# Sixteen pairs of input projection blocks with seven products for eight, and the activation combinations on VectorE alone

## The chip, the cores and the metric

The kernel runs as one program on one core of one Trainium2 chip. The metric is the device time of one execution in microseconds; lower is better. Every time below is one of the runs shown or is read from the profile of one execution. The engines are called by their names in the profile: PE is TensorE (matmul) and PEld its weight load, DVE is VectorE, ACT is ScalarE, POOL is GpSimd, SP is SyncE, which here only issues DMAs.

## The reference

Two requests of 512 tokens each, the prompt and the sample, go through the same layer with the same weights. What matters here is the large input projection, and the convolution that uses part of it:

```python
h = rms_norm(x, norm_g)                                  # 2 x 512 tokens, D_MODEL 1024
proj = jnp.einsum('bsd,de->bse', h, w_in)
c_q, c_kv, k_rope, gate_a, conv_in, gate_c, mg_a, mg_c = split_columns(proj)
# branch A: latent attention of 8 heads, y_a = (attn * silu(gate_a)) @ w_o_attn
# branch C:
u = conv_in[..., :1024] * jax.nn.sigmoid(conv_in[..., 1024:])
u = depthwise_conv(u, kern, width 31) + dw_bias          # along the tokens
u = jax.nn.silu(layer_norm(u, conv_ln_g, conv_ln_b)) * jax.nn.silu(gate_c)
y_c = jnp.einsum('bsc,cd->bsd', u, w_pw2)
merged = jax.nn.sigmoid(mg_a) * y_a + jax.nn.sigmoid(mg_c) * y_c
return x + jnp.einsum('bsd,de->bse', merged, w_out)
```

All of it is float32.

## The kernel before

**Products.** A float32 matrix product is made of three passes in the type fp32r: both operands are split into a high and a low part, and the kernel adds high·high, high·low and low·high. The weight split is a cast on ScalarE (L128, L178) and a subtraction on VectorE or GpSimd (L129, L179).

**Blocks of the input projection.** The activations stand transposed in SBUF as eight k-blocks of 128 channels, `hH[k, b]` and `hL[k, b]`, for batch b = 0 (prompt) and 1 (sample). The projection is made in blocks of 128 output columns. Their names are `ca` and `cb` (the two halves of the convolution's gated input), `ga` and `gc` (the two SiLU gates), `ma` and `mc` (the two merge gates), each with j from 0 to 7. A block alone (`single`, matmuls at L325 into tiles `pbi`) takes 8 k-blocks × 2 batches × 3 passes = 48 matmuls of 512 columns, so two of them take 96. Two blocks together can be made by `seven`, which treats the product as a 2×2 matrix product (k halves by batches by blocks) with seven products of half size in place of eight: 7 × 4 × 3 = 84 matmuls (L356 to L358, tiles `pba`, `pbb`, `pbc`, `pbd`). For that it needs combinations of the weights, formed by `sums` on GpSimd (four adds of 128×512), which with the raw halves give seven splits (`ohi` on ScalarE at L178, `olo` on GpSimd at L179); combinations of the activations, `TH[n, k]` and `TL[n, k]` for n = 1 to 4, formed once at the beginning by `combine_x`; and five additions on the results: `u2` on GpSimd (L376) and `v`, `b`, `c`, `d` on VectorE (L382, L383, L387, L394).

**The start.** The tokens are normed (`norm_x`), transposed on PE into PSUM banks (`trans_x`, L275), and split into `hH` (ScalarE, L306) and `hL` (VectorE, L307) by `evac_x`. The first two blocks, `cb0` and `ca0`, sit in tiles `blk` and run for batch 0 while batch 1 is still being transposed, two banks at a time from the pool `p1`. `whole_x` rebuilds the float32 activations of batch 0 as `xw`. `combine_x(k)` forms, out of `xw` and the transposes of batch 1, `t1` and `t3` on VectorE (L291, L292), `t2` and `t4` on GpSimd (L293, L294), then for each of the four a high part on ScalarE (L298) and a low part on GpSimd (L299). After this the pool of `blk` is closed and PSUM is given to `pb` (6 banks, all `pbi` and `pba` to `pbd` tiles) and `py`. The first `pbi` tile takes the bank that `ca0` occupied, which becomes free with the product u = ca·sigmoid(cb) on VectorE (L494).

**The convolution.** When `ca_j` is done, `take` forms u_j (L494) and queues `conv_ops`: one ScalarE operation that starts y (L406), 30 taps on VectorE (L412, `scalar_tensor_tensor` of 128×1024; the first reads u and y from SBUF, those between accumulate in the PSUM tile `py`, the last writes y), and a DMA of y_j to DRAM (`y_s`, L414, on SP's queue). `drain(n)` puts the next n of these steps into the program between pieces of PE work.

**Order.** The list `plan` sets the order of the units on PE, which is kept as written. On the other engines a scheduler orders the instructions by priorities and modelled times. The weights stream in through three `raw` tiles by DMAs on SP's queue (L115). The last NLN = 6 units are the tail: there `tokens(t)` is woven between the halves of single blocks. It loads y back from DRAM for 128 tokens (`load_tok`: `yt` from `y_s`, L531, and `gt` from `gc_s`, L532), transposes it on PE into `yT` (L537), and does the layer norm and the gates on VectorE and ScalarE. The weights of the `p` projection, attention, and the output projection follow; they take the second half of the span.

Of the kernel before, what the change touches and what calls it, by code (L numbers as in the profile page):

```python
# [9 lines left out]
F32 = mybir.dt.float32  # L10
# [7 lines left out]
P = 128  # L18
D = 1024
S = 512  # L20
NT = 1024
KD = 8
# [21 lines left out]
def encoder_block(tc, xp_d, xs_d, win_d, wkr_d, whd_d, wqr_d, wo_d, wp_d, wout_d, vec_d, dwk_d, rg_d, rc_d, yp_d, ys_d):  # L44
    nc = tc.nc
    opened = {}

    def open_pool(name, **kw):
        if kw.get("space") is not DRAM:
            kw["reuse_waits"] = "tile"  # L50
        cm = tc.tile_pool(name=name, **kw)
        opened[name] = cm
        return cm.__enter__()
# [5 lines left out]
    f = lambda ap: ap.bitcast(F32)  # L59
    mm = nc.tensor.matmul  # L60
    ACT = nc.scalar.activation
    DVE = nc.vector
# [17 lines left out]
    pp = open_pool("pp", bufs=3, space=PSUM)  # L80
# [111 lines left out]


    plan = [("cb", 0), ("ca", 0), ("cb", 1), ("ca", 1), ("ma", 0), ("ma", 1)]
    singles = [("ga", j) for j in range(2, KD)] + [("ma", j) for j in range(2, 6)] + [("mc", j) for j in range(KD)]
    twos = [(("gc", j), ("gc", j + 1)) for j in range(0, KD, 2)] + [(("ga", 0), ("ga", 1))]
    for j in range(2, KD):
        plan.append((("cb", j), ("ca", j)))
        if j % 2 == 0:
            plan += [singles.pop(0), singles.pop(0)]  # L200
        else:
            plan.append(twos.pop(0))
    plan += twos + singles
    NLN = 6
    keys = []
# [66 lines left out]
    def trans_x(b, banks, ks):  # L272
        for tt in range(4):
            for k in ks:
                nc.tensor.transpose(banks[k][:, tt * P : (tt + 1) * P], xt[4 * b + tt][:, k * P : (k + 1) * P], identf)  # L275

    tp = open_pool("hT", bufs=1, side="right")
    TH = {(n, k): tp.tile([P, S], F32R, name=f"tH{n}_{k}") for n in (1, 2, 3) for k in range(4)}
    TL = {(n, k): tp.tile([P, S], F32R, name=f"tL{n}_{k}") for n in (1, 2, 3) for k in range(4)}
    xw = {k: tp.tile([P, S], F32, tag=f"t4_{k}", name=f"xw{k}") for k in range(KD)}  # L280

    def whole_x(k):

        nc.gpsimd.tensor_add(xw[k], f(hH[k, 0]), f(hL[k, 0]))

    def combine_x(k, banks):
        g1, g2 = (vec[:, V_NG + q : V_NG + q + 1] for q in (k, k + 4))
        b22 = xpool.tile([P, S], F32, tag="b22", name=f"b22_{k}")
        t = {n: wp.tile([P, S], F32, tag=f"s{n}", bufs=1, name=f"t{n}_{k}") for n in (1, 2, 3, 4)}
        ACT(b22, banks[k + 4], AF.Identity, scale=g2)  # L290
        DVE.scalar_tensor_tensor(t[1], banks[k], g1, xw[k], op0=ALU.mult, op1=ALU.subtract)  # L291
        DVE.scalar_tensor_tensor(t[3], banks[k], g1, b22, op0=ALU.mult, op1=ALU.subtract)  # L292
        nc.gpsimd.tensor_sub(t[2], b22, t[1])  # L293
        nc.gpsimd.tensor_sub(t[4], xw[k + 4], t[2])  # L294
        TH[4, k] = tp.tile([P, S], F32R, tag=f"t4_{k}", name=f"tH4_{k}")
        TL[4, k] = tp.tile([P, S], F32R, tag=f"t4_{k + 4}", name=f"tL4_{k}")
        for n in (1, 3, 2, 4):
            nc.scalar.copy(TH[n, k], t[n])  # L298
            nc.gpsimd.tensor_sub(TL[n, k], t[n], f(TH[n, k]))  # L299

    def evac_x(b, banks, ks):
        for k in ks:
            g = vec[:, V_NG + k : V_NG + k + 1]
            hi = hp.tile([P, S], F32R, name=f"hH{k}_{b}")
            lo = hp.tile([P, S], F32R, name=f"hL{k}_{b}")
            ACT(hi, banks[k], AF.Identity, scale=g)  # L306
            DVE.scalar_tensor_tensor(lo, banks[k], g, f(hi), op0=ALU.mult, op1=ALU.subtract)  # L307
            hH[k, b], hL[k, b] = hi, lo

    def x_bank(b, k):  # L310
        return p1.tile([P, S], F32, tag="p1", name=f"xT{b}_{k}")
# [121 lines left out]
    banks = {}  # L433
# [18 lines left out]
        block_mm(first[i], i, hh, hl, (0,))  # L452
    for k in range(KD):
        whole_x(k)
    for k in range(4):
        banks = {kk: x_bank(1, kk) for kk in (k, k + 4)}
        trans_x(1, banks, banks)
        evac_x(1, banks, banks)
        combine_x(k, banks)
    for i in (0, 1):  # L460
        block_mm(first[i], i, hh, hl, (1,))
        ensure(3 + i)
# [119 lines left out]
    pp = open_pool("pp", bufs=3, space=PSUM)  # L582
# [335 lines left out]
    ga = stage_a(*units[0])  # L918
# [35 lines left out]
    ga = {1: stage_a(*units[1])}  # L954
    gr = pieces[2:]
    for s_ in range(4 * NU + 3):
        n, j = divmod(s_, 4)
# [46 lines left out]
    pp = open_pool("pp2", bufs=4, space=PSUM)  # L1004
# [131 lines left out]
```

## Time and profile before

| | |
|---|---|
| three runs | 1182.19, 1182.81, 1184.61 us; median 1182.81 us |
| the profiled execution | 1184.55 us |
| its span in the profile | 1182.8 us |
| share of the span busy | PE 97%, DVE 65%, ACT 41%, POOL 29% |
| mean DMA rate | 92 GB/s |

The profile is of one execution, with the span counted from its first to its last instruction; the 1.75 us between span and time lie around it. A row of the trace such as `385.40 76.16 PE pbi L325 x336` is a start, a duration, an engine, a tile and line, and how many instructions it groups; square brackets at a row's end give the idle time of that engine before it and what ended it. The slices of the page cut the span into 40 parts of 29.6 us.

### The profile page before, as it was taken

The page shows a single profiled execution, that of the slowest core. Times are in us where ns is not written, and L with a number is a line of the kernel's source. Part 1 is how long each engine was busy: PE and PEld are TensorE (multiplying, and loading weights), DVE is VectorE, ACT ScalarE, POOL GpSimd, SP SyncE. Part 2 cuts the span into 40 slices and gives each one's busy share as a digit, 9 for nine tenths or more (in the row PEclk, how much of TensorE's full clock was granted, in tenths as well). Part 3 has the DMA queues.
Part 4 walks back from the last instruction along what each step waited for, and adds up shares of the span by engine and source line. Part 5 has one row for each costly group of instructions (what it writes and reads, how often), then busy time and mean ns, then how long its engine had stood idle before and what let it go on. Part 6 is the DMA issues. An engine that isn't in the chain of part 4 may idle for free.

```text
span 1182.8 us, 15035 instructions
## 1 busy us (share of the span) xinstructions
PE 1145.4 (97%) x5856; PEld 969.4 (82%) x5856; DVE 763.1 (65%) x1112; ACT 488.5 (41%) x909; POOL 343.3 (29%) x292
## 2 busy tenths in 40 slices
PE   6689999999999999999999999999999999999998
PEld 4468888888888888877888887899999998888887
DVE  5589899989999962652212454787877789344311
ACT  6522344343343222871101335776676687122200
POOL 5853566586576322200000001322122221000000
PEclk9889999999999999999999999999999999999999
DMA  6011223223223444534343012101100111344431
GB/s 253 1 54 71 71 89 111 86 71 107 89 107 107 160 147 151 158 115 160 138 142 125 23 52 76 39 26 34 35 25 19 36 36 37 107 135 166 161 107 72
DMA packets 46519, 109.52 MB, mean 93 GB/s; under 512 B 3696, under 2 KB 20336, under 8 KB 46448
## 3 DMA queue, kind: packets, MB, share of 16 engines
q1 hardware_dynamic: 41552, 91.78, 23.6%
q10 hardware_dynamic: 4896, 16.78, 3.5%
q8 instruction: 46, 0.75, 0.3%
q14 instruction: 25, 0.20, 0.1%
HBM read 79.18 MB, written 29.36 MB: 92 GB/s over the span
## 4 chain that ended last, share of the span: by engine, by line
PE 92%; POOL 3%; ACT 3%; DVE 1%; issue 1%; DMA 1%; SPq 0%; ACTq 0%; DVEq 0%
PE blk L325 22%; PE pbi L325 20%; PE po L1058 7%; PE pt L825 2%; PE pbd L356 2%; PE pba L356 2%; PE pbb L356 2%; PE pbd L358 2%; PE pba L358 2%; PE pbb L358 2%; PE pbb L357 2%; PE pbd L357 2%; PE pba L357 2%; PE pkv L733 1%; PE pkv L735 1%; PE pkv L734 1%
## 5 line engine op out<-in xcount | busy, mean ns | idle before, releaser
L412 DVE SCALAR_TENSOR_TENSOR py<-u,dwk,py 128x1024 f32<-128x1024 f32 x224 | 288.5, 1288 | 6.2
L128 ACT CAST whi<-raw 128x1024 fp32r<-128x1024 f32 (+3 forms) x59 | 60.5, 1025 | 282.0 <-PE blk L325 165.8
L325 PE MATMUL pbi<-hH,whi 128*128 128x512 f32 x352 | 138.9, 395 | 8.1 <-DVE u L494 8.1
L325 PE MATMUL pbi<-hL,whi 128*128 128x512 f32 x352 | 137.9, 392 | 0.0
L325 PE MATMUL pbi<-hH,wlo 128*128 128x512 f32 x352 | 108.9, 391 | 0.0
L129 DVE TENSOR_TENSOR wlo<-raw,whi 128x1024 fp32r<-128x1024 f32 (+2 forms) x38 | 53.4, 1405 | 59.9 <-ACT whi L128 59.9
L325 PEld LDWEIGHTS pbi<-hH,whi 128*128 128x128 f32 x352 | 66.6, 189 | 22.1 <-DVE u L494 8.5
L325 PEld LDWEIGHTS pbi<-hH,wlo 128*128 128x128 f32 x352 | 66.5, 189 | 14.0
L325 PEld LDWEIGHTS pbi<-hL,whi 128*128 128x128 f32 x352 | 66.7, 190 | 13.6
L179 POOL TENSOR_TENSOR olo<-s,ohi 128x512 fp32r<-128x512 f32 x44 | 57.5, 1318 | 52.7 <-ACT ohi L178 52.7
L129 POOL TENSOR_TENSOR wlo<-raw,whi 128x1024 fp32r<-128x1024 f32 x20 | 48.4, 2418 | 83.5 <-ACT whi L128 83.5
L325 PE MATMUL blk<-a,whi 128*128 128x512 f32 x256 | 68.4, 389 | 0.0
L816 ACT ACTIVATE pr<-sc,nm,sqs 128x512 f32<-128x512 f32 x64 | 51.2, 800 | 28.3 <-DVE nm L814 28.2
L251 POOL TENSOR_TENSOR rk<-sk,mhalf 128x4 f32<-128x4 f32 x16 | 17.2, 1074 | 147.7 <-DVE sk L743 147.7
L325 PE MATMUL blk<-hH,whi 128*128 128x512 f32 x144 | 57.6, 406 | 1.2 <-ACT hH L306 0.7
L325 PE MATMUL blk<-hL,whi 128*128 128x512 f32 x144 | 57.8, 401 | 0.5 <-DVE hL L307 0.4
L178 ACT CAST ohi<-s 128x512 fp32r<-128x512 f32 x44 | 26.2, 620 | 75.2 <-PE pbi L325 51.0
L325 PEld LDWEIGHTS blk<-a,whi 128*128 128x128 f32 x256 | 48.0, 188 | 9.9
L179 POOL TENSOR_TENSOR olo<-raw,ohi 128x512 fp32r<-128x512 f32 x33 | 43.7, 1324 | 35.2 <-ACT ohi L178 26.5
L325 PE MATMUL blk<-cH,whi 128*128 128x512 f32 x128 | 50.7, 396 | 2.4 <-ACT whi L128 2.4
L1061 DVE TENSOR_TENSOR o<-po,xr 128x1024 f32<-128x1024 f32 (+1 forms) x9 | 10.0, 1106 | 64.2 <-PE po L1058 64.2
L603 DVE TENSOR_TENSOR tmc<-blk,smc 128x1024 f32<-128x1024 f32 x8 | 9.8, 1225 | 64.2 <-PE blk L325 64.2
(272 smaller groups left out, 3076.5 us busy)
## 6 DMA issues: line engine op xcount, KB each, us to landing
raw<-in_win_dram SPq DMA_DIRECT2D x53, 512.0 KB, 3.6
y_s<-y SPq DMA_DIRECT2D x8, 512.0 KB, 4.0
ga_s<-stga ACTq DMA_DIRECT2D x8, 512.0 KB, 2.6
gc_s<-stgc ACTq DMA_DIRECT2D x8, 512.0 KB, 2.6
yt<-y_s SPq DMA_DIRECT2D x8, 512.0 KB, 5.3
gt<-gc_s SPq DMA_DIRECT2D x8, 512.0 KB, 4.1
mc_s<-stmc ACTq DMA_DIRECT2D x8, 512.0 KB, 3.4
raw<-in_wp_dram SPq DMA_DIRECT2D x8, 512.0 KB, 5.1
```

Of the source, the lines that this page charges most:

```text
L128: nc.scalar.copy(hv, rv)
L129: (sub or DVE).tensor_sub(lv, rv, f(hv))
L178: nc.scalar.copy(hi[:, sl], src)
L179: nc.gpsimd.tensor_sub(lo[:, sl], src, f(hi[:, sl]))
L325: mm(ps[b] if isinstance(ps, list) else ps[:, b], (wlo if wl_ else whi)[:, k], xl(k, b) if xl_ else xh(k, b), start=(k == 0 and wl_ == 0 a ...
L356: mm(ps, hi[:, k], xh, start=first and k == 0, stop=False, skip_group_check=not first)
L357: mm(ps, hi[:, k], xl, start=False, stop=False, skip_group_check=not first)
L358: mm(ps, lo[:, k], xh, start=False, stop=k == 3, skip_group_check=not first)
L412: DVE.scalar_tensor_tensor(out, u[:, :, i : i + S], dwk[:, j, i : i + 1], src, op0=ALU.mult, op1=ALU.add)
L816: ACT(pr, ps, AF.Exp, bias=nm, scale=r["sq"][:, j : j + 1], accum_out=sm)
L825: nc.tensor.transpose(pt[:, kt], pr[:, kt * P : (kt + 1) * P], identf)
L1058: mm(ps[:, n], lhs[k][:, ts_], w[k][:, n * S : (n + 1) * S], start=first_, stop=last_)
```

## The change

It has three parts. `plan` now makes 16 units by `seven` instead of 11: to the six pairs (`cb_j`, `ca_j`) for j = 2 to 7 and the four of `gc` come all four of `ga` (one before) and two of `mc`. Each of the six pairs is now followed by one such two; before, a pair with even j was followed by two single blocks. Singles in `plan` after the first six units go from 18 to 8 (`ma2` to `ma5`, `mc4` to `mc7`); four twos and two singles stand between the last pair and the tail of six singles, where two twos and six singles stood. In `combine_x` all subtractions of `t2`, `t4` and of the low parts go from GpSimd to VectorE, 24 instructions. And `combine_x(k)` now runs one step behind the transposes; for odd k the two banks of the transposes come from the third tile of the pool `pp` instead of from `p1`. After the change the lines between the old L203 and L449 stand 3 lines earlier, those behind it 4 later.

```diff
     plan = [("cb", 0), ("ca", 0), ("cb", 1), ("ca", 1), ("ma", 0), ("ma", 1)]
-    singles = [("ga", j) for j in range(2, KD)] + [("ma", j) for j in range(2, 6)] + [("mc", j) for j in range(KD)]
-    twos = [(("gc", j), ("gc", j + 1)) for j in range(0, KD, 2)] + [(("ga", 0), ("ga", 1))]
+    singles = [("ma", j) for j in range(2, 6)] + [("mc", j) for j in range(4, KD)]
+    twos = [((nm, j), (nm, j + 1)) for nm, n in (("gc", KD), ("ga", KD), ("mc", 4)) for j in range(0, n, 2)]
     for j in range(2, KD):
         plan.append((("cb", j), ("ca", j)))
-        if j % 2 == 0:
-            plan += [singles.pop(0), singles.pop(0)]
-        else:
-            plan.append(twos.pop(0))
+        plan.append(twos.pop(0))
     plan += twos + singles
     NLN = 6
...
         DVE.scalar_tensor_tensor(t[3], banks[k], g1, b22, op0=ALU.mult, op1=ALU.subtract)
-        nc.gpsimd.tensor_sub(t[2], b22, t[1])
-        nc.gpsimd.tensor_sub(t[4], xw[k + 4], t[2])
+        DVE.tensor_sub(t[2], b22, t[1])
+        DVE.tensor_sub(t[4], xw[k + 4], t[2])
...
         for n in (1, 3, 2, 4):
             nc.scalar.copy(TH[n, k], t[n])
-            nc.gpsimd.tensor_sub(TL[n, k], t[n], f(TH[n, k]))
+            DVE.tensor_sub(TL[n, k], t[n], f(TH[n, k]))
...
-    for k in range(4):
-        banks = {kk: x_bank(1, kk) for kk in (k, k + 4)}
-        trans_x(1, banks, banks)
-        evac_x(1, banks, banks)
-        combine_x(k, banks)
+    held = {}
+    for k in range(5):
+        if k < 4:
+            if k % 2:
+                two = pp.tile([P, 2, S], F32, tag="pp", name=f"xT1_{k}")
+                held[k] = {k: two[:, 0], k + 4: two[:, 1]}
+            else:
+                held[k] = {kk: x_bank(1, kk) for kk in (k, k + 4)}
+            trans_x(1, held[k], held[k])
+            evac_x(1, held[k], held[k])
+        if k > 0:
+            combine_x(k - 1, held[k - 1])
```

**How the order moves.** At three places the prediction rests on it. Names in the rows are tiles with running numbers; `out<-in`.

The first place is VectorE at the end of the start, up to the u of the block `ca0` (`u<-blk,sig`) that frees the first bank of `pb`. Before:

```order
L307 SCALAR_TENSOR_TENSOR hL_1_470<-xT_3_459,vec,hH_1_469 128x512
L307 SCALAR_TENSOR_TENSOR hL_1_474<-xT_7_460,vec,hH_1_473 128x512
L291 SCALAR_TENSOR_TENSOR t_3_478<-xT_3_459,vec,xw_151 128x512
L292 SCALAR_TENSOR_TENSOR t_3_480<-xT_3_459,vec,b_3_477 128x512
L129 TENSOR_TENSOR wlo_555<-raw_552,whi_554 128x1024
L494 TENSOR_TENSOR u_583<-blk_312,sig_580 128x512 x2
L412 SCALAR_TENSOR_TENSOR py_651<-u_583,dwk,y_649 128x1024
```

and after the change, from the last `hL` on:

```order
L304 SCALAR_TENSOR_TENSOR hL_1_452<-xT_3_438,vec,hH_1_451 128x512
L291 TENSOR_TENSOR t_2_459<-xw_154,t_2_457 128x512
L296 TENSOR_TENSOR tL_2_142<-t_2_457,tH_2_130 128x512
L288 SCALAR_TENSOR_TENSOR t_3_476<-xT_3_438,vec,xw_151 128x512
L289 SCALAR_TENSOR_TENSOR t_3_478<-xT_3_438,vec,b_3_475 128x512
L296 TENSOR_TENSOR tL_2_466<-t_2_459,tH_2_465 128x512
L290 TENSOR_TENSOR t_3_477<-b_3_475,t_3_476 128x512
L296 TENSOR_TENSOR tL_3_139<-t_3_476,tH_3_127 128x512
L296 TENSOR_TENSOR tL_3_147<-t_3_478,tH_3_135 128x512
L291 TENSOR_TENSOR t_3_479<-xw_155,t_3_477 128x512
L296 TENSOR_TENSOR tL_3_143<-t_3_477,tH_3_131 128x512
L129 TENSOR_TENSOR wlo_553<-raw_550,whi_552 128x1024
L498 TENSOR_TENSOR u_581<-blk_312,sig_578 128x512 x2
```

All but one of the 24 moved subtractions now stand on VectorE ahead of that u; from the first `hL` of batch 1 to u there are 16 `scalar_tensor_tensor`, 23 such subtractions, one `wlo` and the two u. On GpSimd none of them is left.

The second place is VectorE at the end of the last unit by `seven`, whose last addition is `pbd<-pbd,u`. Before:

```order
L394 TENSOR_TENSOR pbd_2845<-pbd_2845,u_2848 128x512
L412 SCALAR_TENSOR_TENSOR py_2526<-u_2218,dwk,py_2526 128x1024 x5
L412 SCALAR_TENSOR_TENSOR y_2524<-u_2218,dwk,py_2526 128x1024
L412 SCALAR_TENSOR_TENSOR py_2840<-u_2518,dwk,y_2838 128x1024
L412 SCALAR_TENSOR_TENSOR py_2840<-u_2518,dwk,py_2840 128x1024 x28
L412 SCALAR_TENSOR_TENSOR y_2838<-u_2518,dwk,py_2840 128x1024
L542 BN_STATS bst_3464<-yT_3455 128x6 x2
```

After:

```order
L384 TENSOR_TENSOR pbc_3206<-pbc_3206,v_3209 128x512
L409 SCALAR_TENSOR_TENSOR py_2997<-u_2570,dwk,py_2997 128x1024 x3
L391 TENSOR_TENSOR pbd_3205<-pbd_3205,u_3208 128x512
L409 SCALAR_TENSOR_TENSOR py_2997<-u_2570,dwk,py_2997 128x1024 x21
L409 SCALAR_TENSOR_TENSOR y_2995<-u_2570,dwk,py_2997 128x1024
L546 BN_STATS bst_3562<-yT_3553 128x6 x2
```

Behind the last unit by `seven` 36 convolution taps stood, and now 22 stand, ahead of the first layer norm statistics of the tail.

The third place is SP's queue at the same point, where the last y goes out (`y_s<-y`) and the first tokens come back (`yt<-y_s`). Before:

```order
L115 DMA raw_3474<-in_win_dram 128x1024
L414 DMA y_s<-y_2838 128x1024
L521 DMA rg<-in_rg_dram 128x256
L522 DMA rc<-in_rc_dram 128x512
L531 DMA yt_3385<-y_s 128x8x128
L532 DMA gt_3386<-gc_s 128x8x128
L115 DMA raw_3624<-in_win_dram 128x1024
L531 DMA yt_3389<-y_s 128x8x128
```

After:

```order
L115 DMA raw_3722<-in_win_dram 128x1024
L115 DMA raw_3872<-in_win_dram 128x1024
L411 DMA y_s<-y_2995 128x1024
L525 DMA rg<-in_rg_dram 128x256
L526 DMA rc<-in_rc_dram 128x512
L535 DMA yt_3483<-y_s 128x8x128
L536 DMA gt_3484<-gc_s 128x8x128
L535 DMA yt_3487<-y_s 128x8x128
```

The two last weight loads for the tail have moved ahead of the last y, and the first two token loads follow one another. On PE, seven single blocks stood between the last unit by `seven` and the first `yT`, and three stand there now; from the first layer norm on, every engine has its instructions in the order of before.

## The prediction

> **What bounds the kernel now.** I read the page first, for the share of each engine and its course over the span:
>
> ```profile
> PE 1145.4 (97%) x5856; PEld 969.4 (82%) x5856; DVE 763.1 (65%) x1112; ACT 488.5 (41%) x909; POOL 343.3 (29%) x292
> ...
> PE   6689999999999999999999999999999999999998
> ...
> DVE  5589899989999962652212454787877789344311
> ...
> POOL 5853566586576322200000001322122221000000
> PE 92%; POOL 3%; ACT 3%; DVE 1%; issue 1%; DMA 1%; SPq 0%; ACTq 0%; DVEq 0%
> ```
>
> PE is full from the fourth slice on and carries 92% of the chain that ended last. But VectorE is nearly full in the first 14 slices (to 414 us), which are the stretch that changes. So fewer matmuls shorten the time only where VectorE and what hangs on it keep up. Then I asked what PE waits for between 50 and 540 us, followed the chain there, and asked for the clock in single stretches:
>
> ```profile
> PE pbi L325 <- DVE u L494: 8.1, 1, 8.1
> PE blk L325 <- ACT whi L128: 2.4, 1, 2.4
> ...
> 64.88 45.80 PE pbi L325 x192
> ...
> 385.40 76.16 PE pbi L325 x336
> 461.56 0.87 PE yT L537 x8
> ...
> 64.80:69.30 4.50, 4.42 (x11) 3.55 (x12) 3.07 (x4) 1.75 (x2) 2.04 (x2) 0.52 0.60 228
> 533.40:536.70 3.30, 3.19 (x8) 2.54 (x9) 1.22 (x1) 0.06 (x1) 0.00 (x0) 0.50 0.91 297
> 310.00:385.00 75.00, 75.00 (x332) 62.14 (x331) 69.36 (x64) 31.00 (x51) 54.81 (x42) 1.00 0.31 106
> ```
>
> The first two rows are waits (total, times, longest), then come three of the chain (start, duration), then three stretches (PE busy with its matmuls, weight loads, VectorE, ScalarE, GpSimd, the granted clock, DMA share, GB/s). In the whole projection PE waits once, 8.1 us for u at the end of the start, and later 2.4 us for a weight cast. After each wait the clock is about half (0.52, 0.50); elsewhere it is 1.00.
>
> **Fewer matmuls.** Five more pairs save 12 matmuls each, 60. A matmul costs its pitch, 76.16 / 336 = 0.2267 us, not the 389 ns that single ones show, since they overlap. 60 × 0.2267 = **13.6 us** less, if PE stays full. The stretch 310 to 385 is already a row of sevens, with PE busy for 75.00 of 75.00 us, so one seven lasts 84 × 0.2267 = 19.04 us. The change makes the row 16 long, and GpSimd and VectorE must finish their share within 19.04 us each time:
>
> ```profile
> 316.48 1.29 POOL L147 TENSOR_TENSOR s<-raw 128x512 f32<-128x512 f32 x1
> ...
> 335.52 1.29 POOL L147 TENSOR_TENSOR s<-raw 128x512 f32<-128x512 f32 x1
> ...
> 162.47 0.69 DVE L382 TENSOR_TENSOR v<-pa,pbb 128x512 f32<-128x512 f32 x1 [2.40 <-PE pbb L358]
> ...
> 181.51 0.69 DVE L382 TENSOR_TENSOR v<-pa,pbb 128x512 f32<-128x512 f32 x1 [0.25 <-PE pbb L358]
> ...
> 189.67 0.70 DVE L394 TENSOR_TENSOR pbd<-pbd,u 128x512 f32<-128x512 f32 x1 [0.97 <-PE pbd L358]
> ...
> 200.74 0.68 DVE L382 TENSOR_TENSOR v<-pa,pbb 128x512 f32<-128x512 f32 x1
> ```
>
> GpSimd starts its first sum once per 19.04 us; it has 12 operations of about 1.27 us there, 15.2 us. VectorE starts v of a pair at 162.47, of the two behind it at 181.51 (it had waited 0.25 us for PE) and of the next unit at 200.74 (no wait): a pair with 14 taps and two u fills 18.8 of 19.04 us, and a two, which waited 0.97 us for PE at `d`, some 18.2. So both keep pace with little to spare. I charge nothing here; PE's cover is that v is not what it waits for at once, and a lag that grew would be the third rival.
>
> **The start.** The wait of 8.1 us in front of 64.88 is the u that stood behind a weight subtraction:
>
> ```profile
> 32.00 0.75 DVE L307 SCALAR_TENSOR_TENSOR hL<-xT,vec,hH 128x512 fp32r<-128x512 f32 x1 [1.14 <-ACT hH L306]
> 32.67 0.74 DVE L291 SCALAR_TENSOR_TENSOR t<-xT,vec,xw 128x512 f32<-128x512 f32 x1
> 33.33 0.74 DVE L307 SCALAR_TENSOR_TENSOR hL<-xT,vec,hH 128x512 fp32r<-128x512 f32 x1
> ...
> 51.60 0.75 DVE L291 SCALAR_TENSOR_TENSOR t<-xT,vec,xw 128x512 f32<-128x512 f32 x1 [2.21 <-POOL t L293]
> ...
> 56.54 7.09 DVE L129 TENSOR_TENSOR wlo<-raw,whi 128x1024 fp32r<-128x1024 f32 x1 [2.96 <-ACT whi L128]
> 63.55 1.28 DVE L494 TENSOR_TENSOR u<-blk,sig 128x512 f32<-128x512 f32 x2
> ...
> 55.28 2.52 POOL L299 TENSOR_TENSOR tL<-t,tH 128x512 fp32r<-128x512 f32 x2
> 57.76 1.26 POOL L293 TENSOR_TENSOR t<-b,t 128x512 f32<-128x512 f32 x1
> 58.98 2.34 POOL L129 TENSOR_TENSOR wlo<-raw,whi 128x1024 fp32r<-128x1024 f32 x1
> 61.28 1.26 POOL L299 TENSOR_TENSOR tL<-t,tH 128x512 fp32r<-128x512 f32 x1
> ...
> 975.73 1.29 DVE L952 TENSOR_TENSOR a<-attn,a 128x512 fp32r<-128x512 f32 x2
> ...
> L129 DVE TENSOR_TENSOR wlo<-raw,whi x38: 957/1216/7086, 12.5 to 1092.9; 128x1024 fp32r<-128x1024 f32 x29, 128x896 fp32r<-128x896 f32 x8, 128x768 fp32r<-128x768 f32 x1
> ```
>
> That subtraction took 7.09 us, against a median of 1216 ns, while GpSimd worked without a gap from 55.28 to 62.54; it ended 1.1 us behind that, which is about its own normal length. The Trainium skill says why that may be ("GPSIMD Engine Reference", section "8. Key points"): GpSimd shares its SBUF interfaces with VectorE and contends with instructions of two SBUF inputs; the trace agrees here.
>
> After the change VectorE has from 32.00 on, in a row: 16 of its `scalar_tensor_tensor` at a pitch of 0.66 us (32.00, 32.67, 33.33), 10.6; 23 subtractions of two SBUF operands at about 0.61 (half the 1216 ns of a `wlo`; the pair at 975.73 gives 0.64), 14.0; `wlo` 1.2; u 1.3. That is 27.1, so u ends at 59.1 without a gap. GpSimd has nothing in between, so the 7.09 is gone. VectorE will not be gapless, as it takes each high part from ScalarE and the waits of before were 0.5 to 3 us each; I add 0.8 us. PE restarts at 59.9 instead of 64.88: **5.0 us** less. Bounds: 5.8 if gapless (59.1 against 64.88), 3.5 with 2.3 us of gaps. The transposes' new tile and the combination one step later cost PE nothing, as the last `hL` stands about 8 us ahead of u's end, where PE did its last 24 matmuls of `ca0` in 7.87 us before.
>
> **The tail.** PE reaches the first `yT` after three singles, not seven; the tokens it transposes come by a chain that begins with VectorE's last taps:
>
> ```profile
> 385.51 0.70 DVE L394 TENSOR_TENSOR pbd<-pbd,u 128x512 f32<-128x512 f32 x1
> 386.12 6.58 DVE L412 SCALAR_TENSOR_TENSOR py<-u,dwk,py 128x1024 f32<-128x1024 f32 x5
> ...
> 432.48 1.28 DVE L412 SCALAR_TENSOR_TENSOR y<-u,dwk,py 128x1024 f32<-128x1024 f32 x1
> 462.48 1.30 DVE L542 BATCH_NORM_STATS2 bst<-yT 128x6 f32<-128x512 f32 x2 [28.71 <-PE yT L537]
> ...
> 433.79 0.33 SPq L414 DMA_DIRECT2D y_s<-y  x1
> ...
> 438.08 0.38 SPq L531 DMA_DIRECT2D yt<-y_s  x1
> ...
> yt<-y_s SPq DMA_DIRECT2D x1, 512.0 KB, 4.3
> ```
>
> Before, 36 taps run from 386.12 to 433.76, 1.323 us each; y goes out at 433.79; `yt` is issued 4.29 us later, when y has landed, and takes 4.3 us: tokens at 442.4. PE comes at 461.56, so 19.2 us are to spare. After, four singles fewer bring PE 192 × 0.2267 = 43.5 us earlier against that end, and 14 taps fewer bring the tokens 14 × 1.323 = 18.5 us earlier. 19.2 − 43.5 + 18.5 = −5.8: **PE waits 5.8 us** (bounds 5.0 and 6.6, as a landing may differ by 0.8). The last weight load, now ahead of y in SP's queue, needs the tile that GpSimd frees when it splits three blocks ahead: by the order, about 25 us behind the last seven, against 30 for y, so it costs nothing. The VectorE idle of 28.71 us is what is eaten up.
>
> A wait this long also slows the clock. In 64.80 to 69.30 eleven matmuls took 4.42 us where 2.5 were due, 1.9 lost; in 533.40 to 536.70 eight took 3.19 where 1.8 were due, 1.4. I take **1.9 us** (1.4 to 2.1). The Trainium skill ("TensorE: Matmul & The Clock Gate", Part 1) has the clock halved after an idle window of about 3.4 us and whole again after as long a busy one; by it the loss would be 1.7 us, and the half clock after only 2.4 us of wait here differs from it. The start's restart is cold before and after, so that cancels.
>
> **Sum.** −13.6 − 5.0 + 5.8 + 1.9 = −10.9. The profiled execution of 1184.55 us (1182.8 span and 1.75 around) becomes 1173.7. It stands 1.74 above the median of 1182.81, so on the median: **1171.9 us**. By the bounds of the terms, 1169.8 (5.8, 5.0, 1.4) to 1174.4 (3.5, 6.6, 2.1).
>
> **Rivals.**
>
> First, no wait in the tail: something holds PE back before it by as much, or y comes earlier. 1171.9 − 7.7 = 1164.2. For it: 28.71 us of idle on VectorE. Against: the 22 taps are behind the last seven in its own order. 0.07.
>
> Second, the start gains nothing: ScalarE and VectorE hand each high and low part to one another, and the gaps add up to 5 us and more; the row at 51.60 above, 2.21 of waiting for a `t`, shows such a gap. 1171.9 + 5.0 = 1176.9. Against: what that gap waited for was GpSimd, which is now out of the loop. 0.11.
>
> Third, sevens in a row lose a little each: VectorE has 0.2 us to spare in a pair. If each of 16 loses 0.5 us, 8.0 in all: 1179.9. Against: the full row from 310. 0.10.
>
> Fourth, slower: the first tap of each convolution reads u and y from SBUF, as the 7.09 us subtraction read two operands there, and GpSimd now has sums and splits for every unit, not for eleven among singles. Of this the trace has a mild case:
>
> ```profile
> 348.04 2.23 DVE L412 SCALAR_TENSOR_TENSOR py<-u,dwk,y 128x1024 f32<-128x1024 f32 x1
> ...
> 349.13 2.28 POOL L179 TENSOR_TENSOR olo<-raw,ohi 128x512 fp32r<-128x512 f32 x1
> ```
>
> If each of the seven first taps behind the start lost 5.9 us as at 56.54, VectorE would lose 41, of which two sevens' slack of about 0.45 us each takes back 6; PE waits for v and the banks: 1171.9 + 35 = 1206.9. It decides the sign from 10.9 us, about 2.5 us at each. Against: even the row above lost 0.95 us only, as GpSimd pauses several times in 19 us. 0.05.
>
> **Chances.** Forecast 0.64, rivals 0.07, 0.11, 0.10, 0.05, others 0.03. A measurement of this kernel tells about 0.2%, 2.4 us, from no change. The range 1164.0 to 1179.0 takes in the first and second rival and part of the third. Faster 0.89 (all but the fourth and what is left of the third), same 0.05, slower 0.06.
>
> **What would show it.** The profile after should have: PE restarting near 60 us with no `wlo` of 7 us on VectorE ahead of it; 16 rows of v, 19.0 us apart, with no wait of PE between; then a wait of PE at the first `yT` of 5 to 7 us for the load of `yt`, and a half clock of about 4 us behind it. Wrong would be the forecast if v's distance grew beyond 19.2 us, if `wlo` or first taps stretched, or if u came at 63 again.

## The result, and the profile after

The changed kernel took 1172.22 us (median of 4 runs, 1170.4 to 1175.04), the kernel before 1183.35 us (median of 4 runs, 1182.19 to 1184.61). The ratio is 0.9908, 95% interval 0.9882 to 0.9934: faster by 11.1 us. The profiled execution took 1175.04 us with a span of 1173.3 us, 2.8 us above the median; where that comes from is told at the end.

The waits of PE between 50 and 540 us of the changed kernel (total, times, longest):

```profile
PE yT L541 <- DMA yt<-y_s: 4.4, 1, 4.4
PE pbi L322 <- DVE u L498: 3.7, 1, 3.7
PE blk L322 <- ACT whi L128: 2.4, 1, 2.4
```

The wait for u at the start has gone from 8.1 to 3.7 us, and a new wait of 4.4 us stands at the first `yT`, for the load of the tokens. No wait lies between them: the row of 16 sevens has none. VectorE at the end of the start, where the `wlo` is back to a normal length and the subtractions run without a gap:

```profile
32.52 0.75 DVE L304 SCALAR_TENSOR_TENSOR hL<-xT,vec,hH 128x512 fp32r<-128x512 f32 x1 [1.25 <-ACT hH L303]
...
55.70 0.69 DVE L291 TENSOR_TENSOR t<-xw,t 128x512 f32<-128x512 f32 x1
56.30 0.69 DVE L296 TENSOR_TENSOR tL<-t,tH 128x512 fp32r<-128x512 f32 x1
57.25 1.23 DVE L129 TENSOR_TENSOR wlo<-raw,whi 128x1024 fp32r<-128x1024 f32 x1 [0.25 <-ACT whi L128]
59.16 1.29 DVE L498 TENSOR_TENSOR u<-blk,sig 128x512 f32<-128x512 f32 x2 [0.68 <-ACT sig L491]
```

Then the tail. VectorE, from the last addition of the last seven to the first layer norm statistics:

```profile
411.84 0.70 DVE L391 TENSOR_TENSOR pbd<-pbd,u 128x512 f32<-128x512 f32 x1
412.45 27.78 DVE L409 SCALAR_TENSOR_TENSOR py<-u,dwk,py 128x1024 f32<-128x1024 f32 x21
440.26 1.28 DVE L409 SCALAR_TENSOR_TENSOR y<-u,dwk,py 128x1024 f32<-128x1024 f32 x1
450.77 1.30 DVE L546 BATCH_NORM_STATS2 bst<-yT 128x6 f32<-128x512 f32 x2 [9.22 <-PE yT L541]
```

SP's issues of the last y and of the first tokens:

```profile
441.57 0.33 SPq L411 DMA_DIRECT2D y_s<-y  x1
...
444.56 0.38 SPq L535 DMA_DIRECT2D yt<-y_s  x1
```

The chain (start, duration), with the restart at the start and the tail:

```profile
60.51 46.59 PE pbi L322 x192
...
441.57 2.91 DMA y_s<-y
...
444.56 4.10 DMA yt<-y_s
...
448.79 1.94 PE yT L541 x8
450.73 6.22 PE pbi L322 x24
```

And the stretches behind both waits (PE busy, then the other engines; the granted clock is the third number from the end):

```profile
60.40:65.00 4.60, 4.50 (x11) 3.53 (x12) 3.91 (x4) 1.80 (x3) 2.38 (x1) 0.50 0.37 118
448.70:452.00 3.30, 3.21 (x12) 2.95 (x13) 1.23 (x2) 0.00 (x0) 1.52 (x3) 0.51 1.03 340
```

VectorE's last tap ends at 441.54, the first tokens are there at 448.7 (444.56 + 4.10). PE had come 4.4 us earlier, and after the wait its clock is at 0.51: the eight transposes take 1.94 us where they took 0.87 before, the 24 matmuls 6.22 where such a row takes 5.49 at full clock.

### The profile page after: what moved, and what is told of

It is laid out like the page before. It is cut to its first block, busy times and chain, and to the rows that moved or that the text cites. A ratio compares the mean times of both kernels' runs of the same rounds, so it can differ in the third digit from the quotient of the medians.

```text
span 1173.3 us, 15056 instructions
## 1 busy us (share of the span) xinstructions
PE 1136.8 (97%) x5796; PEld 962.9 (82%) x5796; DVE 784.7 (67%) x1156; ACT 504.2 (43%) x944; POOL 365.6 (31%) x318
## 4 chain that ended last, share of the span: by engine, by line
PE 88%; DVE 7%; ACT 2%; DMA 1%; issue 1%; POOL 1%; SPq 0%; ACTq 0%; DVEq 0%
PE blk L322 23%; PE pbi L322 9%; PE po L1062 7%; DVE py L409 4%; PE pbd L355 2%; PE pba L355 2%; PE pbb L355 2%; PE pbd L354 2%; PE pbb L354 2%; PE pba L354 2%; PE pba L353 2%; PE pbd L353 2%; PE pbb L353 2%; PE pt L829 2%; PE pkv L737 1%; PE pkv L738 1%
## 5 line engine op out<-in xcount | busy, mean ns | idle before, releaser
L179 POOL TENSOR_TENSOR olo<-s,ohi 128x512 fp32r<-128x512 f32 x64 | 82.2, 1301 | 21.8 <-ACT ohi L178 21.6
L322 PE MATMUL pbi<-hH,whi 128*128 128x512 f32 x192 | 77.5, 404 | 3.7 <-DVE u L498 3.7
L322 PE MATMUL pbi<-hL,whi 128*128 128x512 f32 x192 | 76.3, 397 | 0.0
L179 POOL TENSOR_TENSOR olo<-raw,ohi 128x512 fp32r<-128x512 f32 x48 | 62.3, 1299 | 37.5 <-ACT ohi L178 27.8
L178 ACT CAST ohi<-raw 128x512 fp32r<-128x512 f32 x48 | 29.8, 621 | 98.1 <-POOL s L154 29.2
L178 ACT CAST ohi<-s 128x512 fp32r<-128x512 f32 x64 | 38.2, 620 | 59.6 <-POOL s L148 21.6
L322 PE MATMUL pbi<-hH,wlo 128*128 128x512 f32 x192 | 60.1, 394 | 0.0
L322 PE MATMUL blk<-cL,whi 128*128 128x512 f32 x128 | 50.3, 393 | 0.0
L322 PE MATMUL blk<-hH,wlo 128*128 128x512 f32 x144 | 49.2, 405 | 0.9 <-DVE wlo L129 0.9
L353 PE MATMUL pba<-hH,ohi 128*128 128x512 f32 x128 | 49.8, 389 | 0.0
```

The lines of the kernel that those rows point to most:

```text
L178: nc.scalar.copy(hi[:, sl], src)
L179: nc.gpsimd.tensor_sub(lo[:, sl], src, f(hi[:, sl]))
L322: mm(ps[b] if isinstance(ps, list) else ps[:, b], (wlo if wl_ else whi)[:, k], xl(k, b) if xl_ else xh(k, b), start=(k == 0 and wl_ == 0 a ...
L353: mm(ps, hi[:, k], xh, start=first and k == 0, stop=False, skip_group_check=not first)
```

## The experiments

All were timed against the kernel before on the same chip: 1183.75 us in the first group, 1184.24 in the second, 1183.91 in the third. Where a place of two traces is compared, its time is counted from the first `hL` of batch 1 (32.00 in the kernel before, 32.52 in the changed one), since the time up to there, in which x is loaded, differs by up to 2 us between executions. Differences in us are of medians, and the ratios, which come from all runs, can put them up to 2 us off.

**The plan alone.** The edit is the first hunk of the change, nothing else.

> The plan with 16 pairs alone, the start as in the kernel before. If the terms are separate and add up, as the forecast says: 60 matmuls less are 13.6 us, the wait at the first yT and the slow clock behind it give back 4.4 and 1.9 us (as the changed kernel's trace shows them), so about 7.3 us less than the kernel before, 1176. The wait for u at the start should stay near 8 us. If a row of 16 sevens needs the activation combinations on VectorE, or the gain is the start's in truth, it is 3 us or less.

1179.11 us, ratio 0.9946 (0.9931 to 0.9962): 4.6 us less by the medians and 6.4 by the ratio, where 7.3 were forecast; the interval reaches from 4.5 to 8.2. The chain of its trace:

```profile
64.01 45.99 PE pbi L322 x192
...
451.47 1.94 PE yT L534 x8
...
511.67 10.71 PE pbi L322 x47
```

and the waits of PE:

```profile
PE pbi L322 <- DVE u L491: 9.5, 1, 9.5
...
PE yT L534 <- DMA yt<-y_s: 4.2, 1, 4.2
```

The wait at the start is still there (9.5), the one in the tail is 4.2, and none lies between. The last piece of the tail starts at 511.67 where it started at 520.14 before: 8.5 us, of which 0.9 is an earlier arrival of x; 7.6 remain, which is the sum of the terms. In this execution 2.8 us of them went behind the tail, in code that is the same (1177.1 − 511.67 against 1182.8 − 520.14), where its clock fell at more places than in the kernel before (last section). So the terms of the plan stand in the trace; the time of its six runs does not by itself tell 4.6 from 7.3.

**The start alone.** The other hunks of the change, with the old plan.

> The new start alone (all combinations on VectorE, one step behind the transposes, odd k in the third tile), the plan with 11 pairs as before. By the forecast's theory PE restarts about 4.4 us earlier, some 0.8 of which a longer slow clock may take back: 3.6 to 5 us less than before, 1178.5 to 1179.8. If the earlier restart is lost again, because VectorE then sets the pace of the convolution and of the tail, there is no difference.

1179.58 us, ratio 0.9952 (0.9934 to 0.9969): 4.2 us less. In its trace PE restarts 27.13 us behind the first `hL`, not 32.88, and the first `yT` is 7.7 us earlier by the same count; 2.0 of these come from the clock, which in this execution did not fall to half behind the wait for u (last section). It is the fastest of the six, 1174.65 us. The earlier restart is not lost again. By the ratios the plan (6.4 us) and the start (5.7 us) add up to 12.1 us, where the changed kernel gained 10.9 in its first group and 12.8 when it was run again.

**The two halves of the start.** First the 24 subtractions on VectorE, but the old loop:

```diff
-        nc.gpsimd.tensor_sub(t[2], b22, t[1])
-        nc.gpsimd.tensor_sub(t[4], xw[k + 4], t[2])
+        DVE.tensor_sub(t[2], b22, t[1])
+        DVE.tensor_sub(t[4], xw[k + 4], t[2])
...
-            nc.gpsimd.tensor_sub(TL[n, k], t[n], f(TH[n, k]))
+            DVE.tensor_sub(TL[n, k], t[n], f(TH[n, k]))
```

> Of the new start only the move of the 24 subtractions to VectorE; the combination stays in step with the transposes, which use two banks as before; the plan as before. The last low part of batch 1 then stands ten rows later on VectorE, about 52.4 us, and PE has some 8 us of ca0 behind it: restart at 62 us, a gain of 2 to 3 us (1180.5 to 1181.5). If the move alone is what counts, the gain is that of the whole new start, about 4 us; if the step behind is what counts, none.

1180.79 us, ratio 0.9964 (0.995 to 0.9979): 3.0 us less, as forecast. Then the other half alone, the combination one step behind (the last hunk of the change), with the subtractions left on GpSimd:

> Of the new start only the combination one step behind the transposes and the third tile; the subtractions stay on GpSimd; the plan as before. GpSimd is as long at work as before, and the weight subtraction of VectorE that took 7.09 us still meets it: restart between 62 and 66 us, a gain of 0 to 2 us (1181.4 to 1183.4). If the wait of before came from the banks of the transposes, and not from GpSimd and VectorE sharing, PE restarts near 60 and 4 us are gained.

1187.84 us, ratio 1.0028 (1.0018 to 1.0037): 4.1 us slower, a miss for both theories. VectorE in its trace:

```profile
48.81 9.03 DVE L129 TENSOR_TENSOR wlo<-raw,whi 128x1024 fp32r<-128x1024 f32 x1 [3.38 <-ACT whi L128]
57.77 0.74 DVE L291 SCALAR_TENSOR_TENSOR t<-xT,vec,xw 128x512 f32<-128x512 f32 x1
58.43 0.73 DVE L292 SCALAR_TENSOR_TENSOR t<-xT,vec,b 128x512 f32<-128x512 f32 x1
66.76 1.29 DVE L501 TENSOR_TENSOR u<-blk,sig 128x512 f32<-128x512 f32 x2 [7.59 <-ACT sig L494]
```

and GpSimd beside it:

```profile
54.28 1.26 POOL L294 TENSOR_TENSOR t<-xw,t 128x512 f32<-128x512 f32 x1
55.51 1.25 POOL L299 TENSOR_TENSOR tL<-t,tH 128x512 fp32r<-128x512 f32 x1
59.23 3.71 POOL L299 TENSOR_TENSOR tL<-t,tH 128x512 fp32r<-128x512 f32 x3 [2.47 <-ACT tH L298]
```

and ScalarE, whose casts stand ahead of the sigmoid in its row:

```profile
58.54 1.80 ACT L298 CAST tH<-t 128x512 fp32r<-128x512 f32 x3 [5.28 <-DVE t L291]
64.20 0.62 ACT L298 CAST tH<-t 128x512 fp32r<-128x512 f32 x1 [3.86 <-POOL t L293]
```

The weight subtraction now stands ahead of the last combination on VectorE and takes 9.03 us. It ends at 57.84, 1.08 us after GpSimd's row without gaps (56.76), and only then does VectorE make the last `t`, on which ScalarE and GpSimd wait; the sigmoid for u comes behind them. In the kernel before, that subtraction also ended 1.09 us behind GpSimd's gapless row of subtractions (63.63 and 62.54). There GpSimd did not pause but went on to six memsets, which have no input tile, and its next subtraction was itself longer than its usual 1.26 us:

```profile
62.49 0.12 POOL L490 MEMSET u<- 128x30 f32 x1
...
62.86 1.90 POOL L299 TENSOR_TENSOR tL<-t,tH 128x512 fp32r<-128x512 f32 x1
```

Each time VectorE's instruction got its own 1.1 us when GpSimd's row of two-operand instructions broke off. So the step behind cost time with the subtractions on GpSimd. With them on VectorE it brings the restart from 29.31 us behind the first `hL` (subtractions alone) to 27.13 (both); the times, 3.0 and 4.2 us, lie too close to tell the two apart by themselves.

**GpSimd takes that one subtraction.** The kernel before with

```diff
-                    split(i, nc.gpsimd if i >= 4 else None)
+                    split(i, nc.gpsimd if i >= 3 else None)
```

> The kernel before with one edit: the subtraction of the fourth weight block, the one that took 7.09 us on VectorE ahead of u, is made on GpSimd. If that row alone held u, u now waits for ScalarE's sigmoid, which ended at 62.1: PE restarts 1.5 us earlier, 1182 to 1183. If GpSimd's work on the combinations holds u by another way (ScalarE's casts wait for it), there is no gain, and the 2.4 us more on GpSimd may even show.

1182.28 us, ratio 0.9981 (0.9969 to 0.9994): 1.6 us less. u now waits for the sigmoid and PE restarts 30.96 us behind the first `hL`, not 32.88. The 7 us did not vanish but struck the next VectorE instruction with two SBUF operands, the first tap (VectorE's rows):

```profile
62.70 1.29 DVE L494 TENSOR_TENSOR u<-blk,sig 128x512 f32<-128x512 f32 x2 [8.00 <-ACT sig L487]
67.33 7.55 DVE L412 SCALAR_TENSOR_TENSOR py<-u,dwk,y 128x1024 f32<-128x1024 f32 x1 [3.34 <-ACT y L406]
```

This tap too ended 1.1 us after a break in GpSimd's row, one of only 0.08 us (73.79 to 73.87). It was harmless there, since nothing on PE waited for it.

**The cover of the 24 subtractions taken away.** The prediction let them run at full pace because GpSimd is idle meanwhile. Here the changed kernel gives GpSimd work again:

```diff
+        rv = rt.rearrange("p a b c -> p (a b c)")
+        for q in range(6):
+            nc.gpsimd.tensor_add(rv[:, 0:S], f(hH[k, 1]), f(hL[k, 1]))
         DVE.tensor_sub(t[2], b22, t[1])
```

> The changed kernel with 24 additions of 128x512 more on GpSimd at the start (six for each combination; their result is overwritten and not used), so that GpSimd works there again while VectorE does its 23 subtractions of two SBUF operands. If VectorE's instructions with two SBUF operands are held off as long as GpSimd runs without a gap, as the 7.09 us of one of them suggest, several groups of up to 7 us each come on top: PE restarts 10 to 20 us later and the time is 1182 to 1192. If the two engines merely slow one another a little, or that row had another cause, it is 0 to 3 us more than the changed kernel.

1184.18 us, ratio 1.0006 (0.9994 to 1.0017): the whole gain of the change is gone, 12 us against the changed kernel (the two were timed on different chips, each beside the kernel before). PE restarts 40.4 us behind the first `hL`, where it was 28.0. The way was another than I had expected. VectorE in the middle of it:

```profile
42.12 0.74 DVE L307 SCALAR_TENSOR_TENSOR hL<-xT,vec,hH 128x512 fp32r<-128x512 f32 x1
...
45.20 1.78 DVE L293 TENSOR_TENSOR t<-b,t 128x512 f32<-128x512 f32 x1
46.91 3.49 DVE L299 TENSOR_TENSOR tL<-t,tH 128x512 fp32r<-128x512 f32 x2
50.32 1.74 DVE L294 TENSOR_TENSOR t<-xw,t 128x512 f32<-128x512 f32 x1
```

and GpSimd, 17 of the additions in a row:

```profile
32.13 28.14 POOL L292 TENSOR_TENSOR rt<-hH,hL 128x512 f32<-128x512 f32 x17 [2.76 <-DVE hL L307]
```

No instruction was held for 7 us. Of the 23 subtractions ahead of u, 16 took 1.1 to 1.8 us, not 0.68, together 13 us more, which is the later restart; the seven others took about 0.68, six of them after GpSimd's row had ended at 65.4. GpSimd's additions took 1.66, not 1.26: the two took turns. Instructions with a PSUM operand (`hL`, 0.74) were not touched.

**The tail: the same steps, half a single later.** Tokens start 24 matmuls (5.44 us) later and everything behind keeps its distance.

```diff
         for n, u in enumerate(tail[1:]):
-            tokens(2 * n)
-            take(*u, single(lambda: tokens(2 * n + 1)))
+            if n > 0:
+                tokens(2 * n - 1)
+            take(*u, single(lambda: tokens(2 * n)))
```

The changed kernel itself was run beside it.

> The changed kernel once more, so that the next three are compared with it on the same chip: about 11 us less than before, 1170 to 1175.

> The changed kernel with every token step of the tail half a single block later (5.44 us of PE work), so that the first yT comes after the load that PE waited 4.4 us for. If that wait and the slow clock of 1.9 us behind it are the price of the tail, both go; at the other end only 5.4 us of matmuls are left behind the last token, whose chain through ScalarE and VectorE took 8.9 us, so 3 to 4.5 us come back there: 1 to 3 us less than the changed kernel. If the tail is bound by its loads all along, the wait only moves to a later token and nothing is gained.

The changed kernel: 1172.39 us, ratio 0.9892 (0.9874 to 0.9911). The shifted one: 1167.18, ratio 0.9854 (0.9838 to 0.9871), 5.2 us less. The wait at `yT` is gone, and the wait at the beginning of the next stage, 2.4 us in the changed kernel, is 3.9 here (waits of PE):

```profile
PE blk L322 <- ACT whi L128: 3.9, 1, 3.9
PE pbi L322 <- DVE u L498: 3.7, 1, 3.7
```

So 1.5 us came back, not 3 to 4.5: I had put ScalarE's chain behind the last token end to end, and a part of it ran beside the wait that was there already.

**The tail: later and closer.** The first token step 5.44 us later, the others three or four k-blocks apart, the last where it was; `single` takes a table that says ahead of which k-block a token step stands.

```diff
...
+        at = [4, 8, 11, 15, 18, 22, 25, 29, 32]
         for n, u in enumerate(tail[1:]):
-            tokens(2 * n)
-            take(*u, single(lambda: tokens(2 * n + 1)))
+            take(*u, single({at[t] - 8 * n: t for t in range(9)}))
```

> The changed kernel with the first token step of the tail 5.44 us of PE work later and the other eight closer together (3 or 4 k-blocks between them, not 4), so that the last stands where it stood. If the wait of 4.4 us and the slow clock behind it (1.9) are a price of the place alone, both are saved: 6 us less than the changed kernel, 1165 to 1167. If loads, ScalarE or VectorE cannot keep a token each 6.5 us, waits come back later and 0 to 3 us are gained.

1166.45 us, ratio 0.9847 (0.9832 to 0.9861): 5.9 us less than the changed kernel. The first `yT` finds its tokens, there is no half clock behind it, and PE's waits in the whole tail are 0.9 us together, none over 0.5. The chain:

```profile
448.20 0.87 PE yT L542 x8
449.08 5.49 PE pbi L322 x24
454.57 0.87 PE yT L542 x8
456.32 4.13 PE pbi L322 x18
```

**A pair more.** 17 sevens, made of `mc4` and `mc5`:

```diff
-    singles = [("ma", j) for j in range(2, 6)] + [("mc", j) for j in range(4, KD)]
-    twos = [((nm, j), (nm, j + 1)) for nm, n in (("gc", KD), ("ga", KD), ("mc", 4)) for j in range(0, n, 2)]
+    singles = [("ma", j) for j in range(2, 6)] + [("mc", j) for j in range(6, KD)]
+    twos = [((nm, j), (nm, j + 1)) for nm, n in (("gc", KD), ("ga", KD), ("mc", 6)) for j in range(0, n, 2)]
```

> The changed kernel with one pair more (17 by seven products; mc4 and mc5 too), so one seven and one single stand ahead of the first yT where three singles stood. 12 matmuls less are 2.7 us. If VectorE's convolution sets the time of the first yT, PE only waits longer there, 7 to 8 us for 4.4, and the time stays that of the changed kernel within 1 us. If PE still sets it, 2.7 us are gained.

1175.45 us, ratio 0.9919 (0.9904 to 0.9934): 3.1 us slower by the medians than the changed kernel with 12 matmuls fewer, though the two intervals overlap; the traces show it more clearly. Its wait of PE at the first `yT`:

```profile
PE yT L541 <- DMA yt<-y_s: 10.3, 1, 10.3
```

and VectorE behind its last seven:

```profile
429.74 0.69 DVE L391 TENSOR_TENSOR pbd<-pbd,u 128x512 f32<-128x512 f32 x1
430.35 10.55 DVE L409 SCALAR_TENSOR_TENSOR py<-u,dwk,py 128x1024 f32<-128x1024 f32 x8
440.93 1.28 DVE L409 SCALAR_TENSOR_TENSOR y<-u,dwk,py 128x1024 f32<-128x1024 f32 x1
```

Its first `yT` comes 418.3 us behind the first `hL`, against 416.0 in the changed kernel run beside it: 2.3 us later, and four additions more on VectorE are 4 × 0.60 = 2.4 us. So the theory that VectorE sets the first `yT` holds, but I had missed that in that case the pair's own additions lengthen VectorE's part. In the changed kernel the path to the first `yT` runs over VectorE, and a pair more shortens PE's part, which no longer counts there.

**17 pairs with later tokens.** The two put together, with the token steps at k-blocks 8, 11, 15, 18, 22, 25, 29, 32 and 36:

> 17 pairs, and the first token step of the tail 10.9 us of PE work later, with 3 or 4 k-blocks between token steps and the last half a single block later than in the changed kernel. The wait of 10.3 us should go, 2.7 us of matmuls are saved against the spread kernel with 16 pairs, and about 1.5 us come back at the end of the tail, as in the shifted kernel: 1164.5 to 1166.5. If VectorE's convolution, which a pair more delays by 2.4 us, still sets the first yT, it is 1167 or more.

1165.41 us, ratio 0.984 (0.9827 to 0.9853): the fastest, 18.5 us below the kernel before. Its 1.0 us on the version with 16 pairs lies inside the intervals of both. The wait of 10.3 is gone; the wait at the next stage is 4.8.

## Why the prediction was right

It said 1171.9 in a range of 1164.0 to 1179.0 and a gain of 10.9 us; measured were 1172.22 and 11.1. Its terms by the trace of the changed kernel:

| term | forecast | measured | from |
|---|---|---|---|
| 60 matmuls fewer | −13.6 | −13.6 | 107.10 to 444.4 is 1488 × 0.2267 us; no wait in it |
| the start | −5.0 | −4.9 | restart less first `hL`: 32.88 before, 27.99 after |
| wait at the first `yT` | +5.8 | +4.4 | waits of PE |
| slow clock behind it | +1.9 | +1.8 | 1.94 − 0.87 and 6.22 − 5.49 |
| clock at the restart | 0 | +0.8 | 46.59 − 45.80 |
| first `hL` | 0 | +0.5 | 32.52 − 32.00 |
| behind the tail | 0 | +1.5 | 664.15 − 662.66 |
| sum | −10.9 | −9.5 | spans: 1173.3 − 1182.8 |

The start came out as summed: VectorE has just two gaps between the first `hL` and u, 0.25 and 0.68 us, 0.9 for the 0.8 of the forecast. The second is a wait for ScalarE's sigmoid, so VectorE's queue was the limit to within 0.7 us. (The forecast read VectorE as nearly full in the first 14 slices; its row has a 5 in the first two, and the start, into which the 24 subtractions went, lies in the second.)

The forecast of the wait at `yT` was too large by 1.4 us, outside its bounds of 5.0 and 6.6: it took the landing of y from the kernel before, 4.29 us from issue to issue, and it took 2.99 here. Taps (last tap ended 29.8 us behind the last seven, as worked out) and load (4.10 for 4.3) were right. The change itself shortened the landing. In the kernel before, SP had issued a weight load at 432.11, 1.7 us ahead of y, and the landing took 4.2 us; in the two other traces with that distance (the start alone, the step behind alone) it took 4.1. Wherever the load was issued 3.0 us or more ahead of y, it took 2.6 to 3.0, and in the changed kernel, where the weight loads moved ahead of y, it was 4.9 us ahead and had landed (no DMA ran in the last 1.4 us before y). That the load is the cause is read from these traces, not tested by itself. The forecast saw that move, but asked only whether it cost something.

The last three rows I had set at nothing. The first `hL` and the stretch behind the tail differ between executions. The clock at the restart does not belong to this execution alone: the 192 matmuls took 45.6 to 46.0 us in the four traces with the combinations left on GpSimd and 46.2 to 46.6 in five of the seven with the whole new start (45.20 and 43.82 in the two others), so the half clock before and after, which I let cancel, did not quite.

The near agreement of the totals is thus in part luck. The named terms give −12.3 us by the trace, the three unnamed ones give 2.8 back; and the two profiled executions stand 1.2 and 2.8 us above their medians, so that their −9.5 us are the −11.1 of the medians. Each named term came within 1.4 us of its own.

The first rival (no wait in the tail) fell with the wait. The second (the start gains nothing) fell with the start alone, 4.2 us. The third (sevens in a row lose a little) fell: PE shows no wait in 16 of them. The fourth had the right mechanism, as the runs with the step behind alone and with GpSimd kept at work show, and the wrong place: the eight first taps took 1.28 to 2.38 us in the changed kernel,

```profile
L409 DVE SCALAR_TENSOR_TENSOR py<-u,dwk,y x8: 1280/1436/2381, 63.5 to 398.7; 128x1024 f32<-128x1024 f32 x8
```

so the worst of them lost 1.1 us; that GpSimd's pauses are what keeps it so small was not tested. With GpSimd kept at work at the start the same mechanism cost 12 us and turned the change into none, so the sign did hang on it: on the 24 subtractions, which I had covered by GpSimd's idleness without a rival that tried the cover.

## What to carry to other kernels

When an engine's share of a stage is near full, count what its queue still holds when the stage ends: here PE's saving of 13.6 us was real, and 6 of it waited at the next stage for convolution taps, y's way through DRAM and a slow clock. Such a price lies in the place of the consumer, not in the amount of work, and moving the first consumer by 5.4 us of other work won it back. Before work is moved between VectorE and GpSimd, look which instructions of VectorE with two SBUF operands will run beside a busy GpSimd: the same subtraction took 1.2, 7.1 or 9.0 us.

## What the runs showed of the hardware

**VectorE beside GpSimd.** VectorE's `wlo` and first taps, 128x1024 with two SBUF operands, were held through several instructions of GpSimd (7.09, 9.03, 7.55 us) and ended 1.1 us after its row of two-operand instructions broke off, but the 128x512 subtractions beside a gapless GpSimd took turns with it (1.1 to 1.8 us). The Trainium skill ("GPSIMD Engine Reference", section "8. Key points") names the contention, and these runs agree; that section does not tell when an instruction is held through and when they alternate, and no run here settles it.

**The clock after a short wait.** The same wait of 3.7 us for u left the clock at half in the changed kernel (11 matmuls in the window above) and at full in the kernel with the start alone:

```profile
58.20:62.70 4.50, 4.50 (x20) 3.73 (x21) 3.87 (x3) 1.70 (x3) 2.40 (x1) 1.00 0.40 130
```

Behind the tail, at three places of code that all these kernels share, the clock falls to about half for a few us or does not: both profiles of the changed kernel have all three, the kernel before has two, the plan alone all three and a fourth, the subtractions alone on VectorE none. The first of the places stands behind the wait of 2.4 us for a weight cast: the prediction's row of the kernel before shows half a clock there, while with the subtractions alone, and with the start alone, 14 matmuls passed in 3.3 us behind the same wait, at 1.00. The same holds between executions of one kernel, by their mean clock: the changed kernel's runs of 1170.4 and 1170.77 us had 0.990, those of 1173.68 and 1175.04 had 0.986 and 0.987. One place in the changed kernel:

```profile
700.00:720.00 20.00, 19.35 (x104) 16.36 (x104) 8.46 (x22) 8.24 (x23) 3.92 (x4) 0.91 0.18 62
```

and the same place in the kernel before:

```profile
711.00:731.00 20.00, 19.24 (x112) 16.35 (x110) 8.47 (x22) 8.72 (x24) 3.92 (x4) 1.00 0.19 64
```

A mean of 0.91 over 20 us is 1.8 us lost. By that, as an estimate, three such places make 5 us, about as much as the four runs of the changed kernel lie apart (4.6), so a term of 2 or 3 us is better read from the place in the trace than from the time. The Trainium skill ("TensorE: Matmul & The Clock Gate", Part 1) says that the window in which PE's activity is watched runs freely and does not begin with the kernel; that fits the chance in it, but no run here shows the window itself.
